# A decoder layer on one core: rotation squares moved behind the tables, a rule for due weight splits, and three final normalizations that overlap

## The chip, the core and the metric

The kernel runs on 1 core of one Trainium2 chip, in fp32. The time is the device time of one execution in microseconds: a median of 1334.62 us over three runs (1333.21, 1334.62 and 1335.36). All times of a profile count from the start of its span.

## The reference

One layer of a hybrid decoder, for a prompt of 1024 tokens and 8 samples of 8 tokens (1088 tokens of width 1024 in all, three chunks of 384, 384 and 320 tokens):

```
h = RMSNorm(x); z = h @ w_in                        # columns: q | k | v | u_ssm | u_pool
A: dilated sliding-window attention, (128,1), (512,4), (2048,16), 8 heads of 64, prompt and cached decode
B: S5 state space, 16 groups, complex diagonal state of 64: h_t = a h_(t-1) + B u_t,
   a = exp(dt a_re) (cos + i sin)(dt a_im); y = Re(C h) + D u; GELU, GLU
C: multi-scale trailing means of 2, 4, 8, 16 positions
x = x + w_out @ [RMSNorm(A) | RMSNorm(B) | RMSNorm(C)]
x = x + w_down(silu(g) * a),  [a | g] = causal_conv3(RMSNorm(x) @ w_up)      # d_ff = 2816
y = RMSNorm(x)
```

## The kernel before, in words

Every fp32 matrix is split into a high and a low part, and each product is made of three matmuls over the parts; the split of a weight (`whl`) is a cast on ScalarE (ACT) and a subtraction on VectorE (DVE). The first phase (`phase_ab`) makes z in tiles of 128 columns by chunk (`dps`, from activations `A`), and weaves the state-space part, the attention, the decode over the cached K and V, the pooling and the output projection into it. The second (`phase_c`) is the feed-forward part. Its up projection has 20 rounds of seven products of 24 matmuls each (a fast matrix scheme: `wW`, `wX`, `wY` are the products in PSUM, `T` and `A` the combined activations), whose parts DVE puts together in `raw`; then the convolution (`cv`), the gate (`th`) and a spill of the result (`hj`). The down projection reads it back (`hst`, `hop`), and the last part (`dn`) is done by chunk, c0, c1, c2, after which `final(c)` normalizes the chunk: sums of squares over partitions by PE (`nps`), mean (`rs_x`), reciprocal root by three Newton steps (`rsqrt`, `rs_y`), a broadcast by PE (`nbc`) that ACT copies (`bs`), and eight outputs `yo`, five by DVE and three by GpSimd (POOL).

The state-space part first makes parameters on POOL (`ssm_params`): powers of a, the squares `ssm_rot` (nine, one after the other, each a complex product `cmul` of six instructions), then scaled input matrices. `ssm_tables` makes from these, for each half of the groups, two tables X (real and imaginary, 3 instructions of 128x512 each on POOL), which PE transposes (`rps`), products on DVE (`s_pn`), small matmuls (`gps`), and E, a table of powers that is doubled step by step with the squares.

The order of each engine's instructions is fixed when the program is built. Parts of the work are generators in a `Driver`; each yields the time at which a model of the engines has its next step ready. After each group of matmuls `tick` lets every generator run that is ready, lowest priority number first: splits of weights have -1 to 0.5 (`uw`, `dw`), the gate 1, the final normalization 1.5, the convolution 3. So an edit at one place also moves what stands around it elsewhere.

Of the kernel before, what the change touches and what calls it, by code (L numbers as in the profile page):

```python
# [6 lines left out]
F32 = mybir.dt.float32  # L7
# [5 lines left out]
P = 128  # L13
# [203 lines left out]
class Driver:  # L217
# [3 lines left out]
    def __init__(self, model):  # L221
        self.model = model
        self.fill = []
        self.psum = 5

    def now(self):
        return self.model.free.get("pe", 0.0)
# [26 lines left out]
    def tick(self):  # L254
        t = self.now()
        while True:
            f = self.pick(t)
            if f is None or f["ready"] > t:
                return
            self.step(f)  # L260

    def until(self, cond):
        while not cond():
# [8 lines left out]
class Body:  # L272
# [233 lines left out]
    def ssm_params(self):  # L506
        nc, g = self.nc, self.nc.gpsimd
# [15 lines left out]
        x, th = new(), new()  # L523
# [4 lines left out]
        nf, r, z, m, m2 = new(), new(), new(), new(), new()  # L528
# [6 lines left out]
        s, c = new(), new()  # L535
# [47 lines left out]
        pr, pi = co, si  # L583
        for k in range(9):
            self.cmul(g, rot[:, k, 0, :], rot[:, k, 1, :], pr, pi, pr, pi, t)
            pr, pi = rot[:, k, 0, :], rot[:, k, 1, :]
        yield None

        cr, ci, nr = new(), new(), new()
# [22 lines left out]
        for g2 in range(2):  # L612
            sl = slice(64 * g2, 64 * g2 + 64)
            g.tensor_copy(cb[sl, 0, :, g2, :], b[sl, 2])
            g.tensor_copy(cb[sl, 1, :, g2, :], cneg[sl])

    def ssm_tables(self, hf):

# [27 lines left out]
        v.tensor_tensor(t5, ai, cr, ALU.mult)  # L646
        v.tensor_tensor(pn[:, 1], pn[:, 1], t5, ALU.subtract)
        E = s_e[:, :1024].rearrange("p (r a c) -> p r a c", r=2, a=4)
        g.memset(E[:, 0, :, 0:1], 1.0)
        g.memset(E[:, 1, :, 0:1], 0.0)  # L650
        yield self.M.ready(rn)
# [1010 lines left out]
    def phase_c(self):  # L1662
        tc, nc, D, M, i = self.tc, self.nc, self.D, self.M, self.i
        v, g, cp = nc.vector, nc.gpsimd, self.cp
        M.LAT = 0.17
        fpc = self.pool(after=[self.dp, self.ap], name="ff", bufs=1)
        self.fp = fp = fpc.__enter__()
        T = [fp.tile([P, NTOK], F32R, name="T%d" % q) for q in range(12)]
# [400 lines left out]
        for p in range(10):  # L2069
# [27 lines left out]
                    D.tick()  # L2097
            if p % 2:
                n["down"] = p // 2 + 1
        self.pt = self.psum_pool("pe", 8)  # L2100
        g.dma_start(self.o["conv"], cvo)


        def final(c, parts):
            t0, w = CH[c]
            tt = self.tok_tiles(c)
            ps = self.pt.tile([P, 512], F32, tag="t", name="nps")
            for pi, p in enumerate(parts):
                yield M.ready(p[:, :w])
                for ti, (a, _) in enumerate(tt):  # L2110
                    nc.tensor.matmul(ps[:, ti:ti + 1], p[:, a:a + 128], self.ones[:, 0:1],
                                     start=(pi == 0 and ti == 0), stop=(pi == len(parts) - 1 and ti == 2))
            for k in (2, 5, 7):
                x = self.X[k][:, t0:t0 + w]
                nc.scalar.activation(x, x, AF.Copy, scale=V[:, V_NF + k:V_NF + k + 1])
            ms = self.small.tile([P, 3, 1], F32, tag="rs_x1", name="rs_x", bufs=2)
            v.tensor_scalar(ms[:, :, 0], ps[:, 0:3], 1.0 / 1024, EPS, ALU.mult, ALU.add)
            y = self.rsqrt(ms.rearrange("p a s -> p (a s)"), P, 3)
            yield M.ready(y)
            bc = self.bcast(c, y)  # L2120
            bs = fp.tile([P, 384], F32, tag="th", name="bs", bufs=1)
            nc.scalar.copy(bs[:, :w], bc[:, :w])
            per = NTOK // w
            out = [ring(0, 4 * c + q, [P, per, w], F32, "yo") for q in range(-(-8 // per))]
            ks = (0, 2, 1, 5, 3, 4, 7, 6)
            for q, k in enumerate(ks):
                x, y = self.X[k][:, t0:t0 + w], out[k // per][:, k % per]
                if k in (2, 5, 7):
                    g.tensor_tensor(y, x, bs[:, :w], ALU.mult)
                else:  # L2130
                    v.scalar_tensor_tensor(y, x, V[:, V_NF + k:V_NF + k + 1], bc[:, :w], ALU.mult, ALU.mult)
                o = k // per
                if all(z // per != o for z in ks[q + 1:]):
# [7 lines left out]
        last = None  # L2141
        for c, (t0, w) in enumerate(CH):
            ss = []
            acc = self.wr[0].rearrange("p a m -> p (a m)")[:, :384] if c % 2 else wr[:, 512:896]
            for m in range(8):
# [10 lines left out]
                if 1 <= m < (5, 5, 4)[c]:  # L2156
# [120 lines left out]
```

## Time and profile before

| | |
|---|---|
| median of three runs | 1334.62 us |
| the profiled execution | 1334.44 us, its span 1332.3 us |
| PE busy | 1258.9 us (94%) |
| DVE busy | 965.4 us (72%) |
| ACT busy | 527.6 us (40%) |
| POOL busy | 339.8 us (26%) |
| mean granted clock of PE | 0.974 |

Busy times are of one engine each and lie side by side. The granted clock is a share of 2.4 GHz, so 0.5 is 1.2 GHz. A timeline row has the start, the time, the engine, the line, the operation, out<-in, the shape and the number of instructions merged; in brackets the idle time of the engine ahead of it, and what ended that. All instructions go through one helper, so all have its line, L188, and are told apart by their tiles.

### The profile page before, as it was taken

The page shows a single profiled execution, that of the slowest core. Times are in us where ns is not written, and L with a number is a line of the kernel's source. Part 1 is how long each engine was busy: PE and PEld are TensorE (multiplying, and loading weights), DVE is VectorE, ACT ScalarE, POOL GpSimd, SP SyncE. Part 2 cuts the span into 40 slices and gives each one's busy share as a digit, 9 for nine tenths or more (in the row PEclk, how much of TensorE's full clock was granted, in tenths as well). Part 3 has the DMA queues.
Part 4 walks back from the last instruction along what each step waited for, and adds up shares of the span by engine and source line. Part 5 has one row for each costly group of instructions (what it writes and reads, how often), then busy time and mean ns, then how long its engine had stood idle before and what let it go on. Part 6 is the DMA issues. An engine that isn't in the chain of part 4 may idle for free.

```text
span 1332.3 us, 26297 instructions
## 1 busy us (share of the span) xinstructions
PE 1258.9 (94%) x10412; PEld 1169.6 (88%) x10412; DVE 965.4 (72%) x1911; ACT 527.6 (40%) x1058; POOL 339.8 (26%) x728
## 2 busy tenths in 40 slices
PE   7889999999999789998999999999999979999996
PEld 7887887767766789988999999999999979999996
DVE  5527766555378862588777878778878999999966
ACT  6212323433244232345454545454544543343333
POOL 7861320300001232372223222323322110001003
PEclk9979999999999879999999999999999989999998
DMA  9321312678963424311232331223132685756303
GB/s 340 105 74 32 79 34 77 221 245 270 347 225 112 91 83 120 118 57 61 88 113 69 94 91 56 78 69 97 49 98 82 180 235 151 181 141 169 115 1 134
DMA packets 85754, 165.94 MB, mean 125 GB/s; under 512 B 10176, under 2 KB 43456, under 8 KB 85632
## 3 DMA queue, kind: packets, MB, share of 16 engines
q1 hardware_dynamic: 81520, 149.68, 34.8%
q0 software_dynamic: 2960, 11.55, 5.0%
q10 hardware_dynamic: 1152, 3.04, 0.7%
q8 instruction: 82, 1.34, 0.4%
q14 instruction: 40, 0.33, 0.1%
HBM read 135.18 MB, written 28.47 MB: 123 GB/s over the span
## 4 chain that ended last, share of the span: by engine, by line
PE 72%; DVE 12%; POOL 7%; issue 4%; DMA 3%; ACT 1%; SPq 0%; POOLq 0%; DVEq 0%; ACTq 0%
PE wX L188 25%; PE dps L188 16%; PE wY L188 13%; PE wW L188 5%; POOL ssm_small L188 3%; DVE X L188 2%; PE pv L188 2%; PE S L188 2%; PE od L188 2%; PE Sp L188 1%; DVE whl L188 1%; PE tp L188 1%; PE yps L188 1%; DVE th L188 1%; POOL X L188 1%
## 5 line engine op out<-in xcount | busy, mean ns | idle before, releaser
L188 PE MATMUL dps<-A,whl 128*128 128x384 f32 (+1 forms) x1896 | 375.2, 346 | 21.2 <-ACT whl L188 6.7
L188 PEld LDWEIGHTS dps<-A,whl 128*128 128x128 f32 x1896 | 321.2, 195 | 44.2 <-issue 21.5
L188 PE MATMUL wX<-T,whl 128*128 128x272 f32 x1440 | 194.5, 290 | 9.3 <-DVE whl L188 8.8
L188 PEld LDWEIGHTS wX<-T,whl 128*128 128x128 f32 x1440 | 186.4, 190 | 11.4 <-DVE whl L188 10.8
L188 DVE SCALAR_TENSOR_TENSOR cv<-raw,vec,cv 128x1104 f32<-128x1104 f32 x88 | 119.3, 1366 | 22.2 <-ACT cv L188 21.9
L188 PE MATMUL wX<-hop,whl 128*128 128x272 f32 x960 | 127.1, 289 | 3.0 <-DVE whl L188 2.2
L188 PE MATMUL wY<-A,whl 128*128 128x272 f32 x960 | 127.4, 288 | 0.0
L188 PEld LDWEIGHTS wX<-hop,whl 128*128 128x128 f32 x960 | 123.3, 189 | 3.8 <-DVE whl L188 2.6
L188 PEld LDWEIGHTS wY<-A,whl 128*128 128x128 f32 x960 | 123.2, 188 | 0.0
L188 ACT CAST whl<-wraw 128x512 fp32r<-128x512 f32 (+1 forms) x96 | 56.8, 599 | 156.4 <-PE dps L188 67.6
L188 DVE TENSOR_TENSOR whl<-uraw,whl 128x512 fp32r<-128x512 f32 x120 | 106.4, 893 | 7.0 <-ACT whl L188 7.0
L188 ACT CAST whl<-uraw 128x512 fp32r<-128x512 f32 x120 | 74.5, 621 | 92.5 <-PE wX L188 48.2
L188 POOL TENSOR_TENSOR th<-th,cv 128x64 f32<-128x64 f32 (+1 forms) x36 | 55.6, 1546 | 116.4 <-DVE th L188 105.1
L188 DVE TENSOR_TENSOR whl<-wraw,whl 128x512 fp32r<-128x512 f32 (+1 forms) x96 | 68.6, 719 | 21.2 <-ACT whl L188 20.5
L188 PE MATMUL wY<-hop,whl 128*128 128x272 f32 x480 | 65.6, 293 | 3.0 <-DVE whl L188 2.9
L188 ACT ACTIVATE P<-P,sm 128x128 f32<-128x128 f32 (+7 forms) x64 | 35.7, 558 | 79.9 <-DVE sm L188 79.8
L188 POOL COPY cvo<-raw 128x2 f32<-128x2 f32 x88 | 32.1, 432 | 134.9 <-DVE raw L188 129.1
L188 PEld LDWEIGHTS wY<-hop,whl 128*128 128x128 f32 x480 | 62.9, 191 | 3.6 <-DVE whl L188 3.4
L188 PE MATMUL wW<-A,whl 128*128 128x272 f32 x480 | 63.2, 288 | 0.0
L188 PE MATMUL wX<-A,whl 128*128 128x272 f32 x480 | 63.2, 288 | 0.0
L188 DVE TENSOR_TENSOR X<-X,wX 128x544 f32<-128x544 f32 x80 | 57.0, 720 | 6.5 <-PE wX L188 6.0
L188 PEld LDWEIGHTS wW<-A,whl 128*128 128x128 f32 x480 | 61.3, 189 | 0.0
(265 smaller groups left out, 2024.2 us busy)
## 6 DMA issues: line engine op xcount, KB each, us to landing
K<-in_ck_dram SPq DMA_DIRECT2D x40, 512.0 KB, 5.3
V<-in_cv_dram SPq DMA_DIRECT2D x80, 256.0 KB, 4.1
uraw<-in_w_up_dram SPq DMA_DIRECT2D x40, 512.0 KB, 4.1
hj<-th SPq DMA_DIRECT2D x20, 544.0 KB, 6.5
hst<-hj SPq DMA_DIRECT2D x20, 544.0 KB, 5.0
hst<-hj POOLq DMA_DIRECT2D x20, 544.0 KB, 6.1
draw<-in_w_down_dram SPq DMA_DIRECT2D x20, 512.0 KB, 5.6
wraw<-in_w_in_dram SPq DMA_DIRECT2D x28, 256.0 KB, 3.1
```

The lines of the kernel that those rows point to most:

```text
L188: return f(*args, **kw)
```

## The change

Four edits. (1) `ssm_params` makes only the first of the nine squares; the eight others come from a new `ssm_rot`, called in the first half's `ssm_tables` after the tables X and the products on DVE. (2) `tick` stops before a step of priority 1 or higher when a step of priority under 0.5 becomes ready within `soon`, which is 0.6 us in `phase_c` and 0 before. (3) `final(c)` is entered as soon as a chunk has begun, takes its squares as they come, and is finished only after the last chunk's matmuls; a later chunk has the lower priority number. It has its own PSUM buffers and c1 its own `bs`. (4) the reciprocal roots of c0 and c1 are made on POOL (14 instructions) in place of DVE (12).

```
+            if f is None or f["ready"] > t or f["prio"] >= 1 and self.urgent(t):
                 return
+    def urgent(self, t):
+        return any(f["prio"] < 0.5 and f["cond"] is None and t < f["ready"] <= t + self.soon for f in self.fill)
...
-        for k in range(9):
-            self.cmul(g, rot[:, k, 0, :], rot[:, k, 1, :], pr, pi, pr, pi, t)
-            pr, pi = rot[:, k, 0, :], rot[:, k, 1, :]
+        self.cmul(g, rot[:, 0, 0, :], rot[:, 0, 1, :], co, si, co, si, t)
...
+    def ssm_rot(self):
+        for k in range(1, 9):
+            pr, pi = rot[:, k - 1, 0, :], rot[:, k - 1, 1, :]
+            self.cmul(self.nc.gpsimd, rot[:, k, 0, :], rot[:, k, 1, :], pr, pi, pr, pi, self.rot_t[:, 0, :])
...
         E = s_e[:, :1024].rearrange("p (r a c) -> p r a c", r=2, a=4)
+        if hf == 0:
+            self.ssm_rot()
...
+        D.soon = 0.6
...
-        self.pt = self.psum_pool("pe", 8)
+        self.pt = self.psum_pool("pe", 4)
-        def final(c, parts):
+        def final(c, parts, npt):
...
-            y = self.rsqrt(ms.rearrange("p a s -> p (a s)"), P, 3)
+            y = self.rsqrt(ms.rearrange("p a s -> p (a s)"), P, 3, c < 2)
...
-                if c < 2:
+                if c < 2 and k not in (2, 5, 7):
                     yield M.free["dve"] - 0.3
...
+                if m == 1:
+                    parts = []
+                    last.append(D.add(final(c, parts, 9 - na), "final", 1.5 - 0.1 * c))
+                if m >= na - 1:
+                    parts.append(acc if m == na - 1 else sq)
-            if last is not None:
-                D.drain(last)
-            last = D.add(final(c, [acc] + ss[(5, 5, 4)[c]:]), "final", 1.5)
-        D.drain(last)
+        for f in last:
+            D.drain(f)
```

On PE, where the state-space tables are transposed, before:

```order
L188 MATMUL dps<-A_76,whl 128x320 x2
L188 MATMUL dps<-A_84,whl 128x320
L188 MATMUL dps<-A_69,whl 128x384 x2
L188 MATMUL dps<-A_77,whl 128x384
L188 MATMUL rps<-ident,X_88 128x128 x8
L188 MATMUL dps<-A_70,whl 128x384 x2
L188 MATMUL dps<-A_78,whl 128x384
L188 MATMUL gps<-ssm_small,X_88 128x32 x2
```

and now:

```order
L188 MATMUL dps<-A_73,whl 128x384 x2
L188 MATMUL dps<-A_81,whl 128x384
L188 MATMUL rps<-ident,X_88 128x128 x8
L188 MATMUL dps<-A_74,whl 128x384 x2
L188 MATMUL dps<-A_82,whl 128x384
L188 MATMUL gps<-ssm_small,X_88 128x32 x2
```

The transposes stand 36 `dps` earlier in PE's order, counted from the broadcast of the third chunk's first normalization ahead of both. On POOL the squares now follow the last step of the second table (`X_88` on the first row is that table, `ssm_pt` a scratch tile):

```order
L188 TENSOR_TENSOR X_88<-ssm_pwr,ssm_bb 128x512
L188 TENSOR_TENSOR X_92<-ssm_pwr,ssm_bb 128x512
L188 TENSOR_TENSOR X_88<-X_88,X_92 128x512
L188 TENSOR_TENSOR ssm_rot<-ssm_rot 128x8
L188 TENSOR_TENSOR ssm_pt<-ssm_rot 128x8
L188 TENSOR_TENSOR ssm_rot<-ssm_rot,ssm_pt 128x8
```

In the up projection the order of DVE has two forms that alternate before. This is the end of a round's convolution in one of them:

```order
L188 SCALAR_TENSOR_TENSOR cv<-raw,vec,cv 128x1104
L188 TENSOR_TENSOR uraw<-uraw 128x512
L188 TENSOR_TENSOR raw<-wW,st 128x272
L188 SCALAR_TENSOR_TENSOR th<-th,cv 128x64
L188 SCALAR_TENSOR_TENSOR th<-th,cv 128x544
L188 SCALAR_TENSOR_TENSOR th<-th,cv 128x480
L188 TENSOR_TENSOR whl<-uraw,whl 128x512
L188 TENSOR_TENSOR raw<-wW,st 128x272
```

and now, in every round:

```order
L188 SCALAR_TENSOR_TENSOR cv<-raw,vec,cv 128x1104
L188 TENSOR_TENSOR whl<-uraw,whl 128x512
L188 SCALAR_TENSOR_TENSOR cv<-raw,vec,cv 128x1104
L188 SCALAR_TENSOR_TENSOR th<-th,cv 128x64
L188 SCALAR_TENSOR_TENSOR th<-th,cv 128x544
L188 SCALAR_TENSOR_TENSOR th<-th,cv 128x480
L188 TENSOR_TENSOR raw<-wW,st 128x272
L188 TENSOR_TENSOR whl<-uraw,whl 128x512
```

The subtraction of the split (`whl<-uraw,whl`) has moved from behind the eviction `raw<-wW` and the gate's three `th` to ahead of the last `cv`. At the end of the program DVE had, around the start of c2's normalization (`rs_x`):

```order
L188 SCALAR_TENSOR_TENSOR yo<-X_11357,vec,nbc 128x384
L188 SCALAR_TENSOR_TENSOR yo<-X_11897,vec,nbc 128x384
L188 TENSOR_SCALAR rs_x<-nps 128x3
L188 TENSOR_SCALAR rs_y<-rs_x 128x3
L188 TENSOR_SCALAR rs_y<-rs_y 128x3
```

where the first two rows and three more of their kind are outputs of c1 (384 columns). Now, after the last step of c2's root:

```order
L188 SCALAR_TENSOR_TENSOR rs_y<-rs_t,rs_y 128x3
L188 SCALAR_TENSOR_TENSOR yo<-X_11607,vec,nbc 128x384
L188 SCALAR_TENSOR_TENSOR yo<-X_11605,vec,nbc 128x320
L188 SCALAR_TENSOR_TENSOR yo<-X_11607,vec,nbc 128x320
L188 SCALAR_TENSOR_TENSOR yo<-X_11899,vec,nbc 128x320
L188 SCALAR_TENSOR_TENSOR yo<-X_11357,vec,nbc 128x320
L188 SCALAR_TENSOR_TENSOR yo<-X_11893,vec,nbc 128x320
L188 SCALAR_TENSOR_TENSOR yo<-X_11899,vec,nbc 128x384
L188 SCALAR_TENSOR_TENSOR yo<-X_11357,vec,nbc 128x384
L188 SCALAR_TENSOR_TENSOR yo<-X_11893,vec,nbc 128x384
```

One output of c1 precedes the outputs of c2 (320 columns) here, and three follow them; one more stands ahead of `rs_x`. On POOL, too, two of c1's outputs now follow those of c2.

## Rows read from the trace of the kernel before

**Rows 1.** Stretches: busy us of each engine, granted clock, DMA share, GB/s.
```profile
62.00:87.00 25.00, 15.55 (x60) 14.64 (x61) 7.93 (x12) 1.16 (x3) 17.34 (x42) 0.59 0.15 49
...
400.00:480.00 80.00, 67.95 (x647) 54.84 (x646) 65.36 (x188) 28.33 (x72) 18.86 (x24) 0.88 0.31 86
...
1286.00:1332.00 46.00, 34.34 (x232) 33.48 (x230) 29.19 (x86) 17.05 (x36) 12.32 (x13) 0.88 0.27 98
```

**Rows 2.** Waits of PE: in all, times, the longest.
```profile
PE wX L188 <- DVE whl L188: 11.1, 9, 2.2
...
PE nbc L188 <- DVE rs_y L188: 6.2, 3, 3.7
```

**Rows 3.** Timeline of PE, 56 to 92 us: start, us, what, [idle <-releaser].
```profile
55.72 5.97 PE L188 MATMUL dps<-A,whl 128*128 128x384 f32 x37
...
67.01 1.30 PE L188 MATMUL dps<-A,whl 128*128 128x384 f32 x3 [5.32 <-DVE k L188]
...
70.49 1.12 PE L188 MATMUL rps<-ident,X 128*128 128x128 f32 x4 [2.19 <-POOL X L188]
...
73.86 1.11 PE L188 MATMUL rps<-ident,X 128*128 128x128 f32 x4 [2.25 <-POOL X L188]
...
86.24 0.49 PE L188 MATMUL vps<-ident,vT 128*128 128x128 f32 x3
```

**Rows 4.** Timeline of POOL, 44 to 74 us.
```profile
46.79 0.20 POOL L188 TENSOR_TENSOR ssm_rot<-ssm_rot 128x8 f32<-128x8 f32 x1
...
57.41 0.20 POOL L188 TENSOR_TENSOR ssm_rot<-ssm_rot,ssm_small 128x8 f32<-128x8 f32 x1
...
68.85 1.59 POOL L188 TENSOR_TENSOR X<-X,X 128x512 f32<-128x512 f32 x1
...
72.54 1.26 POOL L188 TENSOR_TENSOR X<-X,X 128x512 f32<-128x512 f32 x1
```

**Rows 5.** Timeline of PE in the up projection.
```profile
685.13 3.15 PE L188 MATMUL wX<-T,whl 128*128 128x272 f32 x23 [0.99 <-DVE whl L188]
...
688.12 3.18 PE L188 MATMUL wY<-A,whl 128*128 128x272 f32 x24
...
727.25 0.28 PE L188 MATMUL wX<-T,whl 128*128 128x272 f32 x1
...
728.52 3.15 PE L188 MATMUL wX<-T,whl 128*128 128x272 f32 x23 [0.99 <-DVE whl L188]
```

**Rows 6.** Timeline of DVE in the up projection.
```profile
682.58 0.44 DVE L188 TENSOR_TENSOR raw<-wW,st 128x272 f32<-128x272 f32 x1 [3.41 <-PE wW L188]
...
684.40 0.68 DVE L188 TENSOR_TENSOR whl<-uraw,whl 128x512 fp32r<-128x512 f32 x1
...
702.38 2.50 DVE L188 TENSOR_TENSOR whl<-uraw,whl 128x512 fp32r<-128x512 f32 x1
```

**Rows 7.** Timeline of POOL in the up projection.
```profile
701.93 2.39 POOL L188 TENSOR_TENSOR th<-th,cv 128x1024 f32<-128x1024 f32 x1 [0.60 <-DVE th L188]
```

**Rows 8.** Timeline of DVE at the end.
```profile
1314.21 0.15 DVE L188 TENSOR_SCALAR rs_x<-nps 128x3 f32<-128x3 f32 x1
...
1319.05 2.71 DVE L188 SCALAR_TENSOR_TENSOR yo<-X,vec,nbc 128x384 f32<-128x384 f32 x5 [0.92 <-ACT bs L188]
...
1321.68 0.15 DVE L188 TENSOR_SCALAR rs_x<-nps 128x3 f32<-128x3 f32 x1
...
1325.53 2.38 DVE L188 SCALAR_TENSOR_TENSOR yo<-X,vec,nbc 128x320 f32<-128x320 f32 x5 [1.53 <-ACT bs L188]
```

**Rows 9.** Timeline of PE at the end.
```profile
1324.06 0.90 PE L188 MATMUL nbc<-ident,rs_y 128*128 128x128 f32 x3 [3.69 <-DVE rs_y L188]
```

**Rows 10.** Timeline of POOL: a reciprocal root made there, 246 to 256 us.
```profile
251.58 0.20 POOL L188 TENSOR_SCALAR rs_y<-rs_x 128x3 int32<-128x3 int32 x1 [2.02 <-DVE rs_x L188]
...
255.20 0.19 POOL L188 TENSOR_TENSOR rs_y<-rs_t,rs_y 128x3 f32<-128x3 f32 x1
```

**Rows 11.** Timeline of POOL at the end.
```profile
1325.58 2.50 POOL L188 TENSOR_TENSOR yo<-X,bs 128x320 f32<-128x320 f32 x3 [3.56 <-ACT bs L188]
```

More of the change, by code (lines that the diff above doesn't have):

```diff
@@ L224, in __init__ @@
         self.psum = 5
+        self.soon = 0.0
     def now(self):
@@ L257, in tick @@
             f = self.pick(t)
-            if f is None or f["ready"] > t:
+            if f is None or f["ready"] > t or f["prio"] >= 1 and self.urgent(t):
                 return
             self.step(f)
+    def urgent(self, t):
+        return any(f["prio"] < 0.5 and f["cond"] is None and t < f["ready"] <= t + self.soon for f in self.fill)
     def until(self, cond):
@@ L582, in ssm_params @@
         self.rot = rot = self.spool.tile([P, 10, 2, 8], F32, name="ssm_rot")
-        pr, pi = co, si
-        for k in range(9):
-            self.cmul(g, rot[:, k, 0, :], rot[:, k, 1, :], pr, pi, pr, pi, t)
-            pr, pi = rot[:, k, 0, :], rot[:, k, 1, :]
+        self.cmul(g, rot[:, 0, 0, :], rot[:, 0, 1, :], co, si, co, si, t)
+        self.rot_t = tt
         yield None
@@ L615, in ssm_params @@
             g.tensor_copy(cb[sl, 1, :, g2, :], cneg[sl])
+    def ssm_rot(self):
+        rot = self.rot
+        for k in range(1, 9):
+            pr, pi = rot[:, k - 1, 0, :], rot[:, k - 1, 1, :]
+            self.cmul(self.nc.gpsimd, rot[:, k, 0, :], rot[:, k, 1, :], pr, pi, pr, pi, self.rot_t[:, 0, :])
     def ssm_tables(self, hf):
@@ L2099, in phase_c @@
                 n["down"] = p // 2 + 1
-        self.pt = self.psum_pool("pe", 8)
+        self.pt = self.psum_pool("pe", 4)
         g.dma_start(self.o["conv"], cvo)
-        def final(c, parts):
+        def final(c, parts, npt):
             t0, w = CH[c]
             tt = self.tok_tiles(c)
-            ps = self.pt.tile([P, 512], F32, tag="t", name="nps")
-            for pi, p in enumerate(parts):
+            ps = self.pt.tile([P, 512], F32, tag="n", name="nps", bufs=2)
+            for pi in range(npt):
+                yield lambda: len(parts) > pi
+                p = parts[pi]
                 yield M.ready(p[:, :w])
@@ L2111, in final @@
                     nc.tensor.matmul(ps[:, ti:ti + 1], p[:, a:a + 128], self.ones[:, 0:1],
-                                     start=(pi == 0 and ti == 0), stop=(pi == len(parts) - 1 and ti == 2))
+                                     start=(pi == 0 and ti == 0), stop=(pi == npt - 1 and ti == 2))
             for k in (2, 5, 7):
@@ L2117, in final @@
             v.tensor_scalar(ms[:, :, 0], ps[:, 0:3], 1.0 / 1024, EPS, ALU.mult, ALU.add)
-            y = self.rsqrt(ms.rearrange("p a s -> p (a s)"), P, 3)
+            y = self.rsqrt(ms.rearrange("p a s -> p (a s)"), P, 3, c < 2)
             yield M.ready(y)
-            bc = self.bcast(c, y)
-            bs = fp.tile([P, 384], F32, tag="th", name="bs", bufs=1)
+            bc = self.bcast(c, y, self.pt.tile([P, 512], F32, tag="b", name="nbc", bufs=2))
+            bs = cp.tile([P, 384], F32, tag="rms", name="bs", bufs=1) if c == 1 else fp.tile([P, 384], F32, tag="th", name="bs", bufs=1)
             nc.scalar.copy(bs[:, :w], bc[:, :w])
@@ L2140, in phase_c @@
         sqs = [t[:, 384 * k:384 * k + 384] for t in sqs for k in range(2)]
-        last = None
+        last = []
         for c, (t0, w) in enumerate(CH):
@@ L2155, in phase_c @@
                 ss.append(sq)
-                if 1 <= m < (5, 5, 4)[c]:
+                na = (5, 5, 4)[c]
+                if 1 <= m < na:
                     e = self.light(-0.5)
                     e.tensor_tensor(acc[:, :w], ss[0][:, :w] if m == 1 else acc[:, :w], sq[:, :w], ALU.add)
+                if m == 1:
[3 more added lines that the diff above has]
+                    parts.append(acc if m == na - 1 else sq)
                 D.tick()
-            if last is not None:
-                D.drain(last)
-            last = D.add(final(c, [acc] + ss[(5, 5, 4)[c]:]), "final", 1.5)
-        D.drain(last)
+        for f in last:
+            D.drain(f)
         for p in self.psums:
```

## Prediction

> **What bounds the kernel now.** I read the table of engines first: TensorE (PE) is busy for 1258.9 of the span's 1332.3 us, VectorE (DVE) for 965.4. So a change can only pay where PE stands still or runs at half clock. The slices then show where that is, and the windows price it [rows 1]: PE lacks 9.5 us in 62 to 87 us at a granted clock of 0.59, 12.1 us in 400 to 480, and 11.7 us in the last 46. The list of waits [rows 2] names the largest causes late in the program: nine waits for a weight split of DVE (`wX` behind `whl`, 11.1 us), and three for the reciprocal root of a normalization (`nbc` behind `rs_y`, 6.2 us). The timelines are read last, one for each edit; the reader is to see in them who releases a stalled PE, and what that engine did just before.
>
> **Edit 1, the rotation squares.** At 61.69 PE has run out of ready work: it waits 5.32 us for a `k` of DVE, then 2.19 and 2.25 us for the two state-space tables X of POOL, 9.76 us in all [rows 3]. All three go back to one chain. POOL makes the eight later rotation squares, 48 instructions, from 46.79 to 57.61, 10.8 us, and only then begins what leads to the tables, which end at 68.85 + 1.59 = 70.44 and 72.54 + 1.26 = 73.80 [rows 4]. DVE's `k` stood behind products that need POOL's earlier steps of the same chain. With the 48 behind the tables, these end at about 59.6 and 63.0 if POOL's own pace is all that holds them.
>
> PE does not get all of it, because the order moves as well: the eight `rps` transposes now stand 36 `dps` earlier. A `dps` at this place takes 5.97/37 = 0.161 us [rows 3], so PE reaches `rps` at 61.69 - 33 x 0.161 = 56.4 (33 of the 36 ran before the stall). It waits 3.2 us, transposes for 0.5, waits 2.9, and starts the second four at about 63.0 in place of 73.86. The clock has most likely fallen by then, as it had before: four transposes took 1.11 us there, against half that at full speed. From the second four to the `vps` at 86.24 it was 12.4 us, mostly at half clock. The 33 moved `dps` now follow there too. If they come after the clock is back they add 5.3 us: 63.0 + 12.4 + 5.3 = 80.7, a gain of 5.5 us. If they all run at half clock they add 10.6, and the gain is 0.2. If the clock is full throughout, half of the 12.4 goes, and it is 11.7. I take 5.5: the row nearest to it is the same work of before, which ended its slow stretch of itself before `vps`. The squares themselves are needed by the later chain on POOL that makes E; that chain waited for PE's `gps` behind the tables, and the squares (63.0 + 10.8 = 73.8) run while PE makes these. So they cost nothing where they go. In the order, the second half's tables and the GLU come some 7 us of PE work later, and the first decode scores 3 us later; K is fetched into space that the state-space part leaves after the GLU, so a wait of those 4 us, an estimate, can eat part of the gain. This and the changed order of the hand-over to the feed-forward part (400 to 480, where DVE is busy for 65.36 of 80 us) I cannot price from the rows; I set them at 0, with 5 us either way.
>
> **Edit 2, due splits first.** In the up projection PE runs products of 24 matmuls. In every second round one of them starts its first matmul and then stands for the second half of a split: at 727.25 one matmul, the next at 728.52, where the others follow each other in (688.12 - 685.13)/23 = 0.13 us [rows 5]. That loses 1.14 us. Between 685 and 946 there are seven such stalls, one each 43.39 us, so 8.0 us. DVE shows the reason [rows 6]: it sat idle for 3.41 us until the eviction `raw<-wW` at 682.58, then made three `th` of 1.54 us together, and only then the split at 684.40 (0.68 us), which PE already wanted 0.99 us before it ended. In the new order the split stands ahead of the last `cv` and the three `th`, and `raw<-wW` behind all of them, in every round. The 3.41 us of idle time hold what now stands ahead of the eviction: `th` 1.54 and the split 0.68, 2.2 us. So all seven stalls go: 8.0 us. PE is busy on both sides of them, so nothing else waits to take their place at once. The bound below is 0: where POOL's large `th` ran, a split took 2.50 us in place of 0.68 [rows 6], with POOL's 2.39 us beside it [rows 7]; in the new order the split is issued before that `th`, but if it met it, PE would wait as before. The start of the up projection and the change to the down projection are ordered anew by the same rule, with no row that prices it: 3 us either way.
>
> **Edits 3 and 4, the end.** Before, the root of the third chunk (c2) begins at 1321.68, behind five outputs of c1 on DVE (2.71 us); `nbc` follows at 1324.06, the five outputs of c2 at 1325.53 [rows 8 and 9], and POOL's three end at 1325.58 + 2.50 = 1328.08 [rows 11]. In the new order c1's root leaves DVE (from `rs_x` to `nbc` one takes 1324.06 - 1321.68 = 2.38 us there), and one output of c1, not five, stands ahead of c2's root: 4 x 0.54 = 2.2 us. Together 4.5 us at most. Against it stands that a root takes 14 instructions and 255.20 + 0.19 - 251.58 = 3.81 us on POOL [rows 10], 1.4 more, so that c1's broadcast, and PE's sums behind it, come later. I take 3.3: `rs_x` of c2 at 1318.4, its outputs 3.85 us later (as before) at 1322.3. Then the work that was put off follows. DVE: 2.38 + three of c1 at 0.54 = 1326.3. POOL: 2.50 + two of c1 at 1.0 (2.50/3, times 384/320) = 1326.8. The last transfer starts there in place of 1328.08: 1.3 us. Were the put-off outputs free it would be 3.3; were POOL's root slower by its own length beside DVE's work, each of the two roots 3.8, c1's outputs on POOL would end the kernel and it would lose about 1.5.
>
> Work of POOL can hold DVE up: the split of 2.50 us beside POOL's 2.39 shows it for large tiles [rows 6 and 7]; for tiles of three columns, as a root has, no row shows it. The Trainium skill (GPSIMD Engine Reference, section 8, Key points) says that GpSimd shares its SBUF interfaces with VectorE and contends with DVE instructions that have two SBUF inputs; that speaks against two roots on POOL beside DVE's additions. By it the end could lose up to 14 x 0.19 = 2.7 us for a root, by the row's 3.81 us alone it gains 1.3; no run here shows the pair, and the sum goes by the row.
>
> **Sum.** 5.5 + 8.0 + 1.3 = 14.8 us. The profiled execution took 1334.44 us (2.1 more than its span), 0.2 under the median of the runs shown, 1334.62. 1334.4 - 14.8 = 1319.6.
>
> **Rivals.**
> A. The clock does not fall in the state-space tables, since PE stands for 6.1 us in two pieces and not 9.8 in three: 6.2 us more, 1313.4. For it: the longest stand shrinks from 5.32 to 3.2. Against: after the first stand alone three `dps` took 1.30 us, 0.43 each and not 0.161 [rows 3], and two stands of 6.1 us with only four transposes between them are hardly less than that one of 5.3.
> B. The first gain is given back at the fetch of K or at the hand-over in 400 to 480, where DVE and transfers set the pace: only 8.0 + 1.3 remain, 1325.1. For it: 12.1 us of PE are lost there [rows 1], so PE that comes earlier may only wait longer. Against: DVE too starts its work earlier, as most of it hangs on PE.
> C. The rule does not do what it says: the split is still not ready (ScalarE's half or POOL's `th` holds it). Then 5.5 + 1.3: 1327.6. Against: the idle 3.41 us.
> D. Slower. Holding other work back puts the eviction `raw<-wW` behind a split that waits for POOL: 2.50 - 0.68 = 1.82 us in each of 20 rounds, 36 us, with none of the 8.0. 1334.4 + 36.4 - 6.8 = 1364. It decides from 6.8/20 = 0.34 us a round on. Against: the eviction after the 2.50 us split of before came late and no PE row near it has a wait.
> E. The gains and unpriced reorderings cancel: 1334.
>
> **How the numbers follow.** The forecast 0.52 (1315 to 1324 by itself: the unpriced 5 us), A 0.14, B 0.15, C 0.07, D 0.07, E 0.05. 0.2% is 2.7 us, what a measurement of this kernel can tell from no change. The forecast, A, B and C are faster: 0.88; E is the same, 0.05; D is slower, 0.07. The range runs from 1309 (A, with some of the unpriced time on its side) to 1330 (C with some of it against): it leaves out D, E and the tails, under 2 in 10.
>
> **What would show it.** Right: PE's stands for `k` and X shrink from 9.8 to about 6 us and `vps` comes near 81; no `wX` row of the up projection has 0.99 us of idle time, and rounds take 21.1 us; the root of c2 starts some 3 us sooner against the last `dn`, and the last rows of DVE and POOL are outputs of c1. Wrong: a new wait at the first decode scores or in 400 to 480 as long as the first gain; waits of `wW` or `wX` for evictions; a root on POOL that takes far over 3.8 us.

## The result and the profile after

The changed kernel takes 1316.1 us in the median (1313.5 to 1319.8, 4 runs), before 1333.9 in the runs beside it: a ratio of 0.9866, 95% interval 0.9843 to 0.9889, so 15 to 21 us less. The forecast was 1319.6. The profiled execution took 1316.87 us, its span is 1315.1.

The stretches that answer to [rows 1], with the one of the up projection (busy us of PE, PEld, DVE, ACT, POOL, granted clock, DMA share, GB/s):

```profile
62.00:87.00 25.00, 22.70 (x121) 22.64 (x121) 3.88 (x7) 3.02 (x6) 22.65 (x93) 0.76 0.20 66
...
400.00:480.00 80.00, 70.83 (x727) 58.48 (x726) 65.97 (x192) 33.33 (x82) 21.80 (x26) 0.93 0.32 99
...
680.00:1045.00 365.00, 365.00 (x2912) 365.00 (x2912) 306.15 (x464) 180.86 (x346) 73.67 (x165) 1.00 0.28 90
...
1286.00:1315.00 29.00, 16.10 (x120) 15.64 (x118) 16.42 (x43) 9.43 (x21) 12.28 (x24) 0.79 0.42 155
```

The state-space stretch now has 22.70 us of PE's work in place of 15.55, at a clock of 0.76, and the 365 us of the up projection have no gap. The last 29 us have a clock of 0.79. The waits of PE that answer to [rows 2], with the one for the tables:

```profile
PE rps L188 <- POOL X L188: 8.0, 2, 5.3
...
PE nbc L188 <- DVE rs_y L188: 5.8, 2, 3.2
...
PE wX L188 <- DVE whl L188: 3.4, 3, 1.7
```

The nine waits of `wX` for a split are three now. The roots still cost 5.8 us, and the tables, 4.4 us in two waits before, cost 8.0, because PE comes to them earlier. Where the time went is best read from PE's own landmarks, the first row of a product. Ahead of the first `vps`, and ahead of the first `wY`, PE has made the same products in every kernel here, in whatever order. Lengths in the profiled execution of the kernel named; the last two columns have all kernels of this study, those that follow included, without edit 1 (5 of them) and with the whole of it (8), smallest to largest and the mean:

| us | before | changed | edit 1 | edit 2 | edits 3, 4 | edits 1, 2 | without edit 1 | with edit 1 |
|---|---|---|---|---|---|---|---|---|
| start to `vps` | 86.2 | 81.5 | 78.3 | 86.1 | 87.4 | 81.2 | 86.1-87.4, 86.6 | 78.3-82.5, 80.8 |
| `vps` to `wY` | 552.4 | 551.2 | 550.8 | 555.3 | 555.7 | 547.2 | 552.3-555.7, 553.9 | 547.2-551.2, 549.3 |
| up: to the last `wX<-T` | 421.7 | 412.6 | 421.7 | 412.6 | 421.9 | 412.6 | | |
| down: `wX<-hop` to `dn` | 225.7 | 222.3 | 222.3 | 226.6 | 226.0 | 223.2 | 224.5-226.6, 225.5 | 222.2-224.5, 223.1 |
| end: to the end of the span | 46.4 | 47.6 | 46.9 | 46.4 | 47.6 | 46.7 | | |
| span | 1332.3 | 1315.1 | 1319.8 | 1326.9 | 1338.5 | 1310.8 | | |

A column is one execution: those of edit 1 (1321.6 us) and of edits 1, 2 (1312.6) are among the shortest of their runs, that of edits 3, 4 (1340.3) is the longest. Two rows were the prediction's main terms: the first, with 4.8 us, and the up projection, with 9.1. The rows between and behind them, 1.2 and 3.4 us, had stood there as 0 with bounds. The end, forecast to gain 1.3, lost 1.2.

PE around the tables, as [rows 3] show it before:

```profile
60.48 1.12 PE L188 MATMUL rps<-ident,X 128*128 128x128 f32 x4 [5.28 <-POOL X L188]
...
64.30 1.11 PE L188 MATMUL rps<-ident,X 128*128 128x128 f32 x4 [2.69 <-POOL X L188]
...
81.46 0.49 PE L188 MATMUL vps<-ident,vT 128*128 128x128 f32 x3
```

The transposes start ten microseconds sooner and `vps` stands at 81.46, against 80.7 forecast.

DVE at the turn of a round in the up projection, as [rows 6] show it before:

```profile
672.94 0.69 DVE L188 TENSOR_TENSOR whl<-uraw,whl 128x512 fp32r<-128x512 f32 x1 [0.33 <-ACT whl L188]
...
674.83 1.54 DVE L188 SCALAR_TENSOR_TENSOR th<-th,cv 128x64 f32<-128x64 f32 x3
...
676.53 0.44 DVE L188 TENSOR_TENSOR raw<-wW,st 128x272 f32<-128x272 f32 x1 [0.15 <-PE wW L188]
...
676.88 2.12 DVE L188 TENSOR_TENSOR whl<-uraw,whl 128x512 fp32r<-128x512 f32 x1
```

The split at 672.94 is made well ahead of the three `th`; the eviction `raw<-wW` waits 0.15 us for PE, no longer 3.41, and the split of 2.12 us behind it is not yet needed. PE is busy for all 365 us between 680 and 1045, as the window above has it.

### The profile page after: what moved, and what is told of

Same layout as the page of the kernel before. It is cut to its first block, busy times and chain, and to the rows that moved or that the text cites. A ratio compares the mean times of both kernels' runs of the same rounds, so it can differ in the third digit from the quotient of the medians.

```text
span 1315.1 us, 26326 instructions
## 1 busy us (share of the span) xinstructions
PE 1249.0 (95%) x10412; PEld 1164.2 (89%) x10412; DVE 974.8 (74%) x1900; ACT 525.9 (40%) x1049; POOL 319.0 (24%) x752
## 4 chain that ended last, share of the span: by engine, by line
PE 77%; DVE 11%; POOL 6%; issue 3%; DMA 3%; ACT 1%; POOLq 0%; SPq 0%; DVEq 0%; ACTq 0%
PE wX L188 25%; PE dps L188 18%; PE wY L188 13%; PE wW L188 6%; DVE X L188 3%; POOL ssm_small L188 3%; PE pv L188 2%; PE S L188 2%; PE od L188 2%; PE tp L188 1%; PE yps L188 1%; PE dn L188 1%; PE Sp L188 1%; DVE whl L188 1%; DMA V<-in_cv_dram 1%
## 5 line engine op out<-in xcount | busy, mean ns | idle before, releaser
L188 PE MATMUL wX<-T,whl 128*128 128x272 f32 x1440 | 190.9, 288 | 0.9 <-DVE whl L188 0.6
L188 ACT CAST whl<-wraw 128x512 fp32r<-128x512 f32 (+1 forms) x96 | 56.9, 599 | 130.6 <-PE wY L188 46.4
L188 POOL TENSOR_TENSOR th<-th,cv 128x64 f32<-128x64 f32 (+1 forms) x32 | 43.9, 1372 | 108.3 <-DVE th L188 97.9
L188 PEld LDWEIGHTS wX<-A,whl 128*128 128x128 f32 x480 | 61.3, 189 | 0.0
```

Of the source, the lines that this page charges most:

```text
L188: return f(*args, **kw)
```

## The experiments

**Which edit did what.** Three kernels take the edits apart and a fourth leaves out the last two; six or twelve runs each, all on one chip.

```
e1_rot       the kernel before + ssm_rot() behind the tables                  (edit 1)
e2_soon      the kernel before + urgent() in tick, D.soon = 0.6 in phase_c    (edit 2)
e3_final     the kernel before + overlapped final(c), roots of c0, c1 on POOL (edits 3, 4)
e4_rot_soon  the changed kernel - edits 3, 4
```

> The kernel before with the first edit alone (the eight rotation squares behind the tables). Theory, the edits add up where the traces show them: the transposes start 10 us earlier, the first vps comes near 81.5 (before 86.2), and what the whole change lost again at the start of the feed-forward part (a 4.3 us wait for a split at 598 us) belongs to the second edit; so some 5 us remain, 1329 (1327 to 1331). Rival, the hand-over between 400 and 480 us takes the early gain back, whatever comes earlier: 1333 to 1335, with the first vps at 81.5 all the same.

Measured: 1324.1 us against 1335.9 of the runs of before beside it, ratio 0.9923 (0.9897 to 0.9948), so about 10 us, and not 5. The table shows where, for an execution that is one of the shorter: 7.9 us up to `vps`, 1.7 from there to `wY`, 3.4 in the down projection. The rival is wrong: nothing takes the early gain back. Of the theory, the transposes and `vps` came as it said. Its sum did not, and the long wait for a split near 598 us, which it gave to the second edit, stands in this kernel too:

```profile
594.19 6.08 PE L188 MATMUL dps<-A,whl 128*128 128x384 f32 x18 [4.28 <-DVE whl L188]
```

So that wait comes with the order that edit 1 leaves; all eight kernels with the whole of edit 1 have it, at 4.27 to 4.29 us. The stalls of the up projection are all still there, as [rows 5] show them before:

```profile
674.29 0.28 PE L188 MATMUL wX<-T,whl 128*128 128x272 f32 x1
...
675.56 3.14 PE L188 MATMUL wX<-T,whl 128*128 128x272 f32 x23 [0.99 <-DVE whl L188]
```

> The kernel before with the second edit alone (due splits first in the feed-forward part). Theory, it owns all that PE gained between its first wX product and the first dn, 15.3 us, less the wait near 598 us that it brought in, about 3: 1319 to 1322, no 0.99 us wait in the up projection, and shorter waits at the change to the down projection. Rival, only the seven stalls are its work, and the rest (the start of the up projection, 2.8 us, and the change to the down projection, 3.4 us) came from the order that the first edit left behind: 8 to 9 us, 1325 to 1327.

Measured: 1328.8 us, ratio 0.9952 (0.9937 to 0.9967), 6.4 us. The up projection alone takes 9.1 us less, and has no wait left (its window):

```profile
680.00:1045.00 365.00, 365.00 (x2912) 365.00 (x2912) 305.68 (x456) 181.08 (x349) 75.25 (x165) 1.00 0.26 85
```

But around its start PE waits for a split of the first products, 3.90 us in the longest wait here (2.65 before in the longest near it), and from `vps` to `wY` it took 2.9 us more, in the down projection 0.9 (PE's waits between 590 us and `wY` are 8.0 us together, before 5.6; the rest of the 2.9 is less than executions of one order differ by here, 552.4 us in before and 555.7 in the kernel of edits 3, 4):

```profile
617.72 12.67 PE L188 MATMUL dps<-A,whl 128*128 128x384 f32 x59 [3.90 <-DVE whl L188]
```

So both of what I expected fell on the total. The gain of the up projection is edit 2's and no other's: 412.6 in every kernel with it and the whole of edit 1 or none, 421.7 to 422.0 in every one without.

> The kernel before with the third and fourth edit (the overlapped final normalizations, two roots on POOL). Theory, as the trace after shows it: the last transfers are put off more than the root of the third chunk gains, +1.3 us, 1335 (1334.5 to 1336). Rival, the prediction's own term: 1.3 us less, 1332.6; or its best case, 3.3 less.

Measured: ratio 0.9996 (0.9979 to 1.0013): the time can't tell 1.3 us more from 1.3 less. The trace can: the end takes 47.6 us from the first `dn` on, as in the changed kernel, against 46.4 in before and in edit 2's kernel, with the old end. The theory holds there.

> The changed kernel without its third and fourth edit, so the first two alone. Theory: 1.3 us under the changed kernel, 1314.8. Rival, the overlap at the end is worth what was forecast for it: 1.3 us over it, 1317.4.

Measured: 1316.5 us, ratio 0.9851 (0.9826 to 0.9877); the changed kernel has 0.9866 (0.9843 to 0.9889). The intervals overlap almost wholly, so this doesn't decide; its end takes 46.7 us. As far as these intervals tell, the first two edits carry the whole gain.

**The hand-over.** Between the last `od` of the decode part and the last `nps<-ones,sq_p`, the sums of the second normalization, before takes 33.3 us (438.26 to 471.61) and the changed kernel 24.4 (439.67 to 464.11), the kernels of edit 1 and of edits 1 and 2 24.7. I took this for a gain of 8.9 us, and three kernels look for its cause. DVE, before, behind its addition of the first output projection (idle time and releaser in brackets):

```profile
457.81 0.56 DVE L188 TENSOR_TENSOR X<-dps,k 128x384 f32<-128x384 f32 x1 [4.81 <-DMA k<-in_xT_dram]
```

It stood 4.81 us for a row of x. PE in the same stretch:

```profile
462.78 0.81 PE L188 MATMUL pps<-X,vf 128*128 128x320 f32 x2 [3.38 <-DVE X L188]
...
467.27 1.28 PE L188 MATMUL dps<-A,whl 128*128 128x384 f32 x3 [2.64 <-ACT A L188]
```

The next kernel takes away what that addition waits for.

```
-            nc.vector.tensor_tensor(xo, ps, xq[m][:, t0:t0 + n], ALU.add)
+            nc.vector.tensor_tensor(xo, ps, xo if m == 0 and c == 0 else xq[m][:, t0:t0 + n], ALU.add)
```

> The kernel before with one operand of one instruction changed: the first residual addition of the output projection (chunk c0, first 128 features) adds the tile to itself and not to the row of x that is fetched for it, so that it waits for no transfer; that piece of the output leaves the residual out. All orders stay as they are. From the last matmul of the decode outputs (od) to the last sum of squares of the pool part (nps<-ones,sq_p) before took 33.3 us, the changed kernel 24.4. Theory, DVE's queue stood behind this fetch for 4.8 us, and PE's pps behind DVE: 28 to 29 us. Rival, the pool chain on ACT and POOL is as late as the fetch: 32 to 33.5 us, and the 8.9 us came from the other order alone.

Measured, one run: 31.6 us, 1.7 less, and 1335.5 in all. PE there:

```profile
463.26 0.81 PE L188 MATMUL pps<-X,vf 128*128 128x320 f32 x2 [1.31 <-DVE X L188]
...
469.46 1.33 PE L188 MATMUL dps<-A,whl 128*128 128x384 f32 x3 [4.35 <-ACT A L188]
```

The theory fell; 31.6 is just under the rival's 32 to 33.5. PE's wait for `pps` shrinks from 3.38 to 1.31 us, but then PE waits 4.35 in place of 2.64 for ACT's `A`.

```
         pr, pi = co, si
-        for k in range(9):            # all before the tables
+        for k in range(5):            # the other four in ssm_rot(), behind them
```

> The changed kernel with only the last four of the eight squares moved behind the tables; four stay ahead of them (24 instructions, some 5.4 us). Theory, the tables' time is POOL's chain and nothing else: the first transposes at 65 to 66 us (60.5 changed, 70.5 before), the first vps between 82 and 85. Rival, PE's new order alone brought them forward: 60 to 62. The hand-over from od to nps<-ones,sq_p shows whether its gain hangs on the number of squares moved: 24 to 25 us again if it is the order that the edit leaves, 28 or 29 if it follows POOL's time.

Measured, one run: 1321.6 us. PE at the tables, and at the hand-over:

```profile
64.46 1.11 PE L188 MATMUL rps<-ident,X 128*128 128x128 f32 x4 [9.05 <-POOL X L188]
```

```profile
458.51 1.44 PE L188 MATMUL pps<-X,vf 128*128 128x320 f32 x2 [4.55 <-DVE X L188]
```

The transposes start at 64.46: four microseconds after the changed kernel's for four squares kept ahead, so the time of the tables is POOL's. The hand-over takes 33.3 us, as long as before, with the wait of `pps` for DVE back. Neither of my two numbers came. The tables come 6 us sooner than before and the hand-over takes the same 33.3, so 24.4 or 33.3 goes with the order that the planner writes, not with POOL's time. With all eight moved, DVE's first residual addition stands behind the second chunk's pooling chain; with four moved, it stands ahead of that chain, as before. This kernel's up projection took 414.9 us with edit 2 in it: the round's exact form varies with what precedes it.

The last of the three is the kernel before with that one addition moved.

```
+            def late():
+                yield self.M.free["dve"] + 3.0
+                nc.vector.tensor_tensor(xo, ps, xq[m][:, t0:t0 + n], ALU.add)
+                nc.scalar.activation(acc, xo, AF.Square)
+            if m == 0 and c == 0:
+                res0.append(D.add(late(), "res0", 2))
+                return
+            if m == 1 and c == 0:
+                D.drain(res0[0])
             nc.vector.tensor_tensor(xo, ps, xq[m][:, t0:t0 + n], ALU.add)
```

> The kernel before, with one difference at the hand-over: VectorE's addition of the first output projection, and the square behind it, wait in the planner's queue, so that they stand behind the second chunk's pooling chain (the maxima of the attention's pooling) and no longer ahead of it; the other edits are left out. Theory: the place of this one addition carries most of the 8.9 us that the changed kernel gains there, because VectorE no longer stands 4.8 us with the whole chain behind it: the hand-over takes 24 to 27 us, the whole 1325 to 1330. Rival: the place of the addition matters by the 1.7 us of the fetch and little more, and the rest comes from the other instructions that stand elsewhere: 30 to 33 us, the whole 1331 to 1337.

Measured, one run: 31.1 us, and 1333.7 in all: the rival. DVE and PE:

```profile
462.33 0.56 DVE L188 TENSOR_TENSOR X<-dps,x 128x384 f32<-128x384 f32 x1 [0.76 <-DMA x<-in_xT_dram]
```

```profile
459.98 0.81 PE L188 MATMUL pps<-X,vf 128*128 128x320 f32 x2 [1.58 <-DVE X L188]
...
461.71 1.30 PE L188 MATMUL dps<-A,whl 128*128 128x384 f32 x3 [0.92 <-DVE X L188]
```

The addition now waits 0.76 us and not 4.81, PE's two waits are 1.58 and 0.92 for 3.38 and 2.64, and still only 2.2 us come of it; up to `wY` nothing is left (552.3). So the stand of DVE was not the 8.9 us. What was, the windows of the two stretches show, for the rows of the tile `dps` alone, before and changed (us, then busy us and count of PE, PEld, DVE, ACT; clock):

```profile
438.26:471.61 33.35, 21.20 (x90) 17.72 (x90) 2.21 (x6) 0.00 (x0) 0.84 0.36 78
```

```profile
439.67:464.11 24.44, 14.53 (x76) 12.61 (x76) 1.67 (x5) 0.00 (x0) 0.98 0.34 96
```

The stretch has 14 `dps` less; in the written order nine stand ahead of it now and six behind it (15, a record is missing). Six `nps` stand ahead of it now too, and forty `pv` of the attention, which stood ahead of it before, stand in it. At before's 21.20/90 = 0.236 us each the 14 `dps` are 3.3 us that went elsewhere. The other 76 take 0.191 us each, at a clock of 0.98 for 0.84: 3.4 us. PE's idle time there goes from 8.3 to 5.1 us, and its other products take 0.9 more: together the 8.9. In this pair the neighbours pay most of it: from `vps` to the last `od` PE takes 358.2 us for 352.0, and from the last `nps<-ones,sq_p` to `wY` 168.5 for 167.0. Between the landmarks that do hold the same work, `vps` and `wY`:

```profile
86.24:638.64 552.40, 524.76 (x4863) 442.62 (x4862) 347.35 (x896) 192.31 (x450) 128.63 (x262) 0.98 0.42 135
```

```profile
81.46:632.62 551.16, 521.43 (x4863) 441.02 (x4862) 350.56 (x905) 189.41 (x440) 131.85 (x255) 0.98 0.43 137
```

The same 4863 rows of PE take 521.43 us for 524.76; PE's idle time, 27.64 us before (552.40 less 524.76), is 29.73 now. So the 1.2 us that are left in this pair are clock and not waits.

The pair overstates what the neighbours pay. The changed kernel's 358.2 us up to the last `od` are the longest of the eight kernels with edit 1 (the others 352.9 to 356.5), and before's 352.0 are among the shortest of the five without (the others 351.4 to 355.7). In the means of the same kernels (`e5_nofetch` and `e12_late` among them) the hand-over takes 24.8 us for 32.6, the stretch ahead of it 2.0 us more and the one behind it 1.2 more: 3.2 of 7.8 us are paid back, and 4.6 stay. Of these PE's own rows are 3.4 (521.2 us for 524.6) and its idle time 1.2 (28.1 for 29.3), so most of it is clock here too. Why the clock is higher with edit 1, no run shows.

**The end.** DVE and POOL at the end of the changed kernel, as [rows 8], [rows 10] and [rows 11] show them before:

```profile
1301.27 0.16 DVE L188 TENSOR_SCALAR rs_x<-nps 128x3 f32<-128x3 f32 x1
...
1305.22 3.96 DVE L188 SCALAR_TENSOR_TENSOR yo<-X,vec,nbc 128x320 f32<-128x320 f32 x8 [1.04 <-ACT bs L188]
```

```profile
1281.00 0.19 POOL L188 TENSOR_SCALAR rs_y<-rs_x 128x3 int32<-128x3 int32 x1 [4.69 <-DVE rs_x L188]
...
1284.92 0.36 POOL L188 TENSOR_TENSOR rs_y<-rs_t,rs_y 128x3 f32<-128x3 f32 x1
...
1305.27 4.42 POOL L188 TENSOR_TENSOR yo<-X,bs 128x320 f32<-128x320 f32 x5 [3.61 <-ACT bs L188]
```

Counted from the first `dn` (1267.45; before 1285.92), c2's root begins at 33.8, 1.9 us sooner than before's 35.8; 3.3 had been forecast. What holds it has changed. Before, PE's sums of c2 end at 1320.37 and the root waits 1.31 us more, behind DVE's outputs; now it begins 0.04 us after the sums, which end at 1301.23 (the last rows of PE's sums, before and changed):

```profile
1317.55 2.82 PE L188 MATMUL nps<-ones,sqs 128*128 128x1 f32 x24
```

```profile
1299.83 1.40 PE L188 MATMUL nps<-ones,sqs 128*128 128x1 f32 x12
```

So 1.27 of the 1.94 us come from DVE's queue, and the other 0.67 are sums that end sooner after the first `dn`. A root on POOL takes 4.28 us here (1281.00 to 1285.28), 0.5 more than [rows 10]: two of its steps take 0.53 and 0.36 us in place of 0.23 and 0.20, each beside an addition of DVE that reads two SBUF tiles (`wraw<-wraw,sqs`) and takes its usual 0.56. That is the pair that the prediction had no row for; it costs 0.3 us (c1's root, 4.08) to 0.5 (c0's) and not 2.7. The last outputs end at 41.7 (DVE) and 42.2 (POOL), against 42.0 and 42.2 before, but the span ends at 47.6 and not 46.4. (In the six kernels with the old order of the end it ends at 46.4 to 47.0, in the three with the new one at 47.6.) The transfers of the last 17 us, before and after, in 40 slices of 0.4 us each (GB/s, then packets and bytes):

```profile
GB/s 0 0 0 0 0 0 0 0 0 0 0 0 351 358 376 343 379 365 358 376 369 379 47 0 0 0 0 343 392 392 395 404 392 389 371 9 0 0 0 0
DMA packets 2160, 2.88 MB, mean 170 GB/s; under 512 B 112, under 2 KB 2160, under 8 KB 2160
```

```profile
GB/s 0 0 0 25 369 340 383 369 351 34 0 0 0 0 228 365 329 4 0 253 395 404 392 395 389 389 401 402 398 390 401 380 358 379 137 0 0 0 0 0
DMA packets 2705, 3.68 MB, mean 216 GB/s; under 512 B 144, under 2 KB 2704, under 8 KB 2704
```

Before, the queue ends with a burst of eight or nine slices that carries c2 alone. After, the put-off outputs of c1 are in the same burst, 14 slices at 358 to 404 GB/s: the queue is full for nearly twice as long. Counted from the first `dn`, the last transfer was issued at 42.18 and landed at 45.41 before, 3.23 us later; now it is issued at 42.51 and lands at 46.65, 4.14 us later. So 0.3 of the 1.2 us that the end loses are a later issue, and 0.9 are the queue.

```
-                    nc.sync.dma_start(self.o["y"][:, per * o:e, t0:t0 + w], out[o][:, :e - per * o])
+                    if c != 1 or o == 0:
+                        nc.sync.dma_start(self.o["y"][:, per * o:e, t0:t0 + w], out[o][:, :e - per * o])
```

> The changed kernel without the last three output transfers of the second chunk (768 of its 1024 features are computed and not written). From the first dn to the end of the span the changed kernel took 47.7 us, before 46.4, though DVE's and POOL's last outputs ended within 0.2 us of before, counted from the same point. Theory, these three transfers queue with the third chunk's and set the end: 46.3 to 46.8. Rival, the end is the last transfer's own time, whatever else is under way: 47.4 to 47.8.

Measured, one run: the end takes 44.8 us, 2.8 less than in the changed kernel, with every engine's outputs at the same times. The transfers of its last 14 us, in slices of 0.35 us:

```profile
GB/s 0 0 0 0 0 136 369 355 356 382 373 272 28 0 0 0 0 0 263 369 369 123 0 0 260 399 402 391 384 402 399 391 380 333 4 0 0 0 0 0
```

The theory is right that these three transfers set the end, and its number is not: 44.8 is 1.5 us under its range. The third chunk's last transfer lands at 43.57 here and at 43.61 in the changed kernel, so the three do not hold it up; they land behind it, at 44.58, 45.60 and 46.65 in the changed kernel. Without them the sooner root does show, as 46.4 - 44.8 = 1.6 us. The put-off outputs cost the 2.8.

```
-            ks = (0, 2, 1, 5, 3, 4, 7, 6)
+            ks = (2, 5, 7, 0, 1, 3, 4, 6) if c == 1 else (0, 2, 1, 5, 3, 4, 7, 6)
+            if c == 2:
+                yield M.ready(bs[:, :w]) + 0.6
```

> The changed kernel with another order of the last outputs: the second chunk's three outputs on POOL go first, and its outputs on DVE into the gap in which the third chunk's broadcast is made, so that nothing of the second chunk follows the third's. Theory, with the transfers of the second chunk out of the way the earlier root shows in the end: from the first dn to the end of the span 45.0 to 45.8 us (47.7 changed, 46.4 before), 1314 us, some 2 us under the changed kernel. Rival, the outputs in the gap put off the third chunk's by as much: 46.5 to 47.7, 1316.

Measured: 1316.7 us, ratio 0.9841 (0.9812 to 0.9869), the same as the changed kernel within the intervals; its end takes 49.3 us. The rival's direction is right, and the price is higher. DVE during c2's root, and POOL beside it:

```profile
1302.53 0.92 DVE L188 TENSOR_SCALAR rs_y<-rs_y 128x3 int32<-128x3 int32 x1
...
1303.48 0.91 DVE L188 TENSOR_TENSOR rs_t<-rs_y 128x3 f32<-128x3 f32 x1
```

```profile
1299.56 4.81 POOL L188 TENSOR_TENSOR yo<-X,bs 128x384 f32<-128x384 f32 x5
```

Two steps of the root take 0.92 and 0.91 us and not 0.17 and 0.16, while POOL writes five outputs of 384 columns (two of c0 and three of c1). The root needs 3.8 us in place of 2.3, and from the last output to the end it takes 6.2 us for the changed kernel's 5.4. The Trainium skill's GPSIMD Engine Reference (section 8, Key points) has GpSimd contend with DVE instructions that are in a 2-port mode or have two SBUF inputs; the second of these two steps reads two, the first reads one, and no run shows in which mode that ran. In this trace it is DVE that pays, 1.5 us in a root, beside large tiles of POOL.

Then the roots were put back, or moved alone.

```
e9_root_dve    -            y = self.rsqrt(..., P, 3, c < 2)
               +            y = self.rsqrt(..., P, 3, False)      # changed kernel otherwise
e10_pool_root  edits 1, 2 and 4; final(c) as before
e11_dve_gap    e8_gap with the line of e9_root_dve
```

> The changed kernel with all three reciprocal roots on DVE, as before (the fourth edit undone, the third kept). Theory: a root on POOL is 1.5 us slower and stood behind a 0.9 us addition there, so the second chunk's broadcast comes some 3 us earlier without it, more of that chunk's outputs are written before the third's, and the tail from the first dn to the end of the span is 46 to 47 us (47.6 changed, 46.4 before). Rival, the root of the second chunk on DVE puts off the additions that the third chunk's sums wait for by its 2.3 us: 48 or more.

> The kernel before with the first, second and fourth edit (roots of the first two chunks on POOL, the final normalizations one after the other as before). Theory: the second chunk's outputs come 1.5 us or more later and all stand ahead of the third chunk's root, so nothing is gained: a tail of 46.5 to 48 us. Rival, the 2.3 us that DVE is rid of bring the third root forward by as much: 44 to 45 us.

Measured, one run each: ends of 51.9 and 49.8 us (1322.0 and 1317.2 in all). For the first the rival is right: c1's root on DVE puts off DVE's additions, PE waits 0.79 us for one of them, and makes c2's sums late and slowly:

```profile
1299.57 1.15 PE L188 MATMUL dn<-hl,whl 128*128 128x320 f32 x6 [0.79 <-DVE X L188]
...
1301.71 4.78 PE L188 MATMUL nps<-ones,sqs 128*128 128x1 f32 x24
```

In the second c1's broadcast waits for POOL, and the same follows; both theory and rival were too low:

```profile
1298.54 0.54 PE L188 MATMUL nbc<-ident,rs_y 128*128 128x128 f32 x3 [1.68 <-POOL rs_y L188]
...
1299.51 5.07 PE L188 MATMUL nps<-ones,sqs 128*128 128x1 f32 x24
```

The 24 `nps` of c2 took 2.82 us before and take 4.78 and 5.07 here. The granted clock was 0.53 from 1302 to 1307 us in the one and 0.50 from 1302 to 1305 in the other, so at 1.2 GHz. That is not the new order's doing alone: in four kernels with the old order of the end (edit 1, edit 2, `e5_nofetch`, `e12_late`) they took 3.85 to 4.73 us, and the ends were 46.4 to 47.0. What these two have beside it is that the sums begin later, 33.3 and 34.0 us after the first `dn` for 31.6.

> The changed kernel with all roots on DVE, and the second chunk's outputs ahead of the third's (on POOL first, on DVE in the gap of the third chunk's broadcast). In the run before with this order and roots on POOL, the third root took 3.8 us on DVE and not 2.3, since five outputs of POOL ran beside it. Theory: with the second chunk's broadcast some 3 us earlier POOL is done with its outputs when the third root starts, so that it takes 2.3 us again, and the transfers are spread: a tail of 44.5 to 46 us, 1313 to 1315 us in all. Rival, POOL's outputs still meet the third root or the additions of the third chunk come later: 47 us or more, 1316 or more.

Measured: 1318.4 us, ratio 0.9875 (0.9857 to 0.9892), an end of 49.2 us: the rival. DVE, and the window of PE's sums ahead of it:

```profile
1299.58 0.16 DVE L188 TENSOR_SCALAR rs_x<-nps 128x3 f32<-128x3 f32 x1 [2.39 <-PE nps L188]
...
1301.83 2.18 DVE L188 SCALAR_TENSOR_TENSOR yo<-X,vec,nbc 128x384 f32<-128x384 f32 x4
```

```profile
1297.00:1300.00 3.00, 2.55 (x12) 2.46 (x12) 0.54 (x4) 0.00 (x0) 2.44 (x3) 0.50 0.73 262
```

The root takes 2.3 us again (1299.58 to 1301.91), since POOL is done, and four outputs of the earlier chunks fill the gap behind it; but it starts late, since DVE waits 2.39 us for the sums, made at a clock of 0.50. And PE's broadcast follows the root by 1.2 us, because it waits for an output of DVE and not for the root:

```profile
1303.11 0.87 PE L188 MATMUL nbc<-ident,rs_y 128*128 128x128 f32 x3 [3.56 <-DVE yo L188]
```

No order of the end that I tried beats before's 46.4 us while it writes everything.

## Why the prediction was right, and where it was not

**The time and the direction** came out right, 17.8 us less for 14.8 forecast, inside the range. The sum was nearer than its parts, and that is luck: the end came out 2.5 us worse than forecast, and what edit 1 gained in the stretches set at 0 made up for it and more.

**Edit 1 at the tables**: 4.8 us for 5.5, by the steps forecast. PE reached `rps` at about 55.2 (60.48 less 5.28), for 56.4; the tables ended 0.8 and 1.2 us later than POOL's shift alone would have them, so the waits are 8.0 and not 6.1 us. The clock fell and came back, and the moved `dps` follow mostly at full speed. The size rests on when the clock comes back: the prediction chose 5.5 out of 0.2 to 11.7, and over eight executions the gain is 4 to 8 us, 5.8 in the mean. Rival A did not come here, but it is alive in part (below).

**Edit 1 later on**: "I set them at 0, with 5 us either way". From `vps` to `wY` it gained 4.6 us between the means, inside that bound, and 1.2 in the pair of the two profiles; no run shows a mechanism for it beyond the higher clock. The down projection, for which the prediction had 3 us either way under edit 2, gained 2.4 between the means: 215.3 us of PE's work in the changed kernel for 217.2, of the same products, and 215.2 for 217.1 in the means, so again mostly clock. With 5.8 up to `vps` this makes 12.8 for edit 1, where its own runs allow 7 to 14. Rival B had looked for a loss here, and none came.

**Edit 2**: the stalls went as the rows said, 9.1 us for 8.0. The seven stalls of 1.14 us make 8.0 of it; the other 1.1 I have not placed. That the rule also costs 2.4 us of waits at the start of the up projection is seen only in the kernel that has it alone; with edit 1 the waits there are the same with the rule and without it (6.5 and 6.4 us). Rivals C and D did not come: no eviction is late.

**The end**: the wrong sign. The step that failed is "The last transfer starts there in place of 1328.08: 1.3 us". The last outputs were to end 1.3 us sooner and ended as late as before (42.2 us after the first `dn`), because the sooner root was over-sized, 1.9 for 3.3: the "4.5 us at most" counted DVE's queue, and of that only the 1.3 us between the end of PE's sums and the root could be had. And the time from the last output to the end was taken as fixed, 4.2 us. It was 5.4, because the put-off outputs of c1 share the queue, 3.68 MB in the last 17 us for 2.88. It is 4.2 in all seven kernels that are done with c1's outputs before PE's broadcast for c2, and 5.3 to 6.2 in the six that are not.

## What to carry to other kernels

Measure an edit of a planned order between landmarks that have the same work ahead of them, count the rows between, and take more than one execution: a stretch that was 8.9 us shorter in one pair seemed to have left 7.7 of them to its neighbours, and in the means of thirteen kernels it was 3.2 of 7.8. Idle time in front of a waiting instruction shows whether work that stands behind it, and is due, fits ahead of it. At the end of a kernel the outputs that are put off are also transfers that are put off, and a full queue gives back what a sooner last step gains.

## What was not expected of the hardware

With the same order of PE up to there, the granted clock came back at different times in the tables' stretch. The changed kernel, and the kernel with edit 1 alone:

```profile
66.00:70.00 4.00, 4.00 (x18) 4.00 (x16) 0.00 (x0) 0.03 (x1) 3.48 (x21) 0.50 0.00 0
...
74.00:78.00 4.00, 4.00 (x27) 4.00 (x26) 1.92 (x3) 1.24 (x2) 3.69 (x13) 0.99 0.08 17
```

```profile
66.00:70.00 4.00, 4.00 (x27) 4.00 (x26) 0.56 (x1) 0.00 (x0) 3.45 (x21) 0.80 0.00 0
...
74.00:78.00 4.00, 4.00 (x25) 4.00 (x24) 1.12 (x2) 0.00 (x0) 3.61 (x18) 1.00 0.07 16
```

In both PE had stood for 4.9 to 5.3 us and then worked at 1.2 GHz (0.50). From 66 to 70 us it still does in one, and is at 0.80 in the other, with no wait of PE in between; only from 74 on are both at 2.4 GHz. So `vps` stands between 78.3 and 82.5 us in eight executions of that order: 4 us that no instruction explains (the first transposes start at 59.9 to 60.8 in all eight), a quarter of the whole change. The 0.16 us steps of a root that take 0.92 beside POOL's outputs were the other surprise.
